# 128 bytes of padding ahead of the weights' pool in a two-layer decoder trunk

## The chip, the cores and the metric

The kernel runs on one core of one Trainium2 chip. The metric is the device time of one execution in microseconds. Three runs of the kernel before took 1982.12 to 1982.59 us, the median is 1982.57 us.

## What is computed

Two layers over x of 512 tokens by 1024 features, in float32. Each layer adds half a SwiGLU, then a mixer, then half a SwiGLU; each works on the RMS-normed x.

```python
for l in range(DEPTH):
    h = _rmsnorm(x, ffn_pre_norm[l])
    x = x + 0.5 * _swiglu(h, ffn_pre_w_gate[l], ffn_pre_w_up[l], ffn_pre_w_down[l])
    h = _rmsnorm(x, mix_norm[l])
    if l % 2 == 0:
        x = x + _retention_dilated_mixer(h, ab_w_in[l // 2], ab_w_out[l // 2])
    else:
        x = x + _gla_mixer(h, gla_w_in[l // 2], gla_w_a2[l // 2], gla_b_a[l // 2], gla_w_out[l // 2])
    h = _rmsnorm(x, ffn_post_norm[l])
    x = x + 0.5 * _swiglu(h, ffn_post_w_gate[l], ffn_post_w_up[l], ffn_post_w_down[l])
return _rmsnorm(x, final_norm)
```

`_swiglu(h, wg, wu, wd)` is `(silu(h @ wg) * (h @ wu)) @ wd` with 2816 hidden features. The even mixer is retention and dilated attention, the odd one is gated linear attention; both begin with a projection of h and end with one of their concatenated heads.

## The kernel before

The 512 tokens lie along the free dimension, 128 features at a time along the partitions. x is 8 tiles of 128 x 512 (`keep`). Before each block `scaled` makes gain times x as a pair of fp32r tiles, `xgh` and `xgl`, whose sum is the float32 value; the row scale of the norm comes after the projection. Weights are loaded by SyncE's queue into `wraw` (128 x 1024, two buffers, 512 KB each) and split by `load_w` into `whi` (ScalarE, L89) and `wlo` (VectorE, L90), four buffers each; `weights` keeps up to three sets ahead of their use.

Every large product goes through `mm3`: for one 128-deep slice, three matmuls into one PSUM bank, high by high (L124), high by low (L125), low by high (L126). The first operand of a matmul (`lhsT`, 128 x 128) is stationary and is loaded into the array ahead of it; the second (`rhs`, 128 x 512) moves through it. In the profile's rows a matmul is written as output, moving tile, stationary tile: `pj<-xgh,whi` has `xgh` moving.

- `proj_steps` (SwiGLU's gate and up, most of the mixers' input): one weight tile of 128 x 1024 gives 128 outputs in 8 x 3 matmuls; its stationary slices lie 512 bytes apart; `xg` moves.
- `proj_n_steps` (the mixers' values): `xg` is stationary in slices of 128 tokens, halves of a weight tile move.
- `down` (the SwiGLU's second product): 22 x 3 matmuls for each of 8 output tiles; `acth` and `actl`, the split activations, move. The last output tile of the kernel is made in two halves of 256 tokens (`last_half`).
- `out_steps` (the mixers' output): `cath` and `catl` move.

The stages run in this order: SwiGLU, even mixer, SwiGLU, SwiGLU, odd mixer, SwiGLU. In each SwiGLU 44 output tiles of projections (gate and up, 22 each) come ahead of the 8 of `down`. In the mixers the projections of later heads are woven into the attention work by hand (`weave`, `fill`), and the norm's statistics are put off and issued between products (`hook`; `rows` makes the row scale with `diag` moving and `ones_r` stationary). The even mixer projects 8 + 8 + 4 tiles with `proj_steps`, the odd one 1 + 8 + 8.

The pools are laid out one after the other in each partition of SBUF, in the order in which `__init__` (L47) opens them: `const`, `keep`, `xg`, `wpool`, `misc`, and after those the pool of the stage that runs. In the program as built the tiles start at these bytes of a partition (several buffers of a tile follow each other at 2048 or 4096 bytes):

| tiles | first byte | modulo 2048 |
|---|---|---|
| `ones_r` | 17024 | 640 |
| x | 18304 | 1920 |
| `xgh`, `xgl` | 34688, 51072 | 1920 |
| `wraw`, `whi`, `wlo` | 67456, 75648, 92032 | 1920 |
| `diag`, `rrow`, `sq` | 108640, 112736, 118880 | 96 |
| `acth`, `actl` (each SwiGLU) | 135488, 180544 | 320 |
| `cath`, `catl` (even mixer) | 185664, 202048 | 1344 |
| `cath`, `catl` (odd mixer) | 191488, 207872 | 1024 |

The even mixer's pool is the largest and ends at byte 228672.

Of the kernel before, what the change touches and what calls it, by code (L numbers as in the profile page):

```python
# [45 lines left out]
class Trunk:  # L46
    def __init__(self, ctx, tc, a):  # L47
        self.tc, self.nc, self.a = tc, tc.nc, a
        pool = lambda name, **kw: ctx.enter_context(tc.tile_pool(name=name, **kw))
        self.const = pool("const", bufs=1)  # L50
        self.keep = pool("keep", bufs=1)
        self.xg = pool("xg", bufs=KD)
        self.wpool = pool("wpool", bufs=4)
        self.misc = pool("misc", bufs=1)
        self.n = 0
        self.plan, self.ready, self.pending = [], [], []
# [5 lines left out]
    @contextmanager  # L62
    def banks(self, **tags):
        """The PSUM banks of a phase, by purpose."""
        with self.tc.tile_pool(name=self.uid("ps"), bufs=1, space=PSUM, reuse_waits="tile") as self.ps:
            self.tags = tags
            yield
# [7 lines left out]

# [1 line left out]
    def weights(self):  # L77
        """The next weights of the plan, in halves."""
        while self.plan and len(self.ready) <= LOOK:
            self.ready.append(self.load_w(*self.plan.pop(0)))  # L80
        return self.ready.pop(0)
# [11 lines left out]
    def hook(self):  # L93
        """One of the steps put off, if any."""
        if self.pending:
            with self.tc.issue_after(self.last):
                self.pending.pop(0)()

    def fill(self, filler, us):
        """Of the filler, about this much work for the tensor engine."""  # L100
        while us > 0:
            t = next(filler, None)
            if t is None:
                return
            us -= t
# [4 lines left out]

# [1 line left out]
    def halves(self, pool, tag, src, bufs):  # L112
        """src (an SBUF or PSUM tile) as two parts of 12 significant bits each."""
        nc = self.nc
        hi = self.t2k(pool, tag + "h", F32R, bufs)
        lo = self.t2k(pool, tag + "l", F32R, bufs)
        nc.scalar.copy(out=hi, in_=src)  # L117
        nc.vector.tensor_tensor(out=lo, in0=src, in1=hi.bitcast(F32), op=ALU.subtract)  # L118
        return hi, lo

    def mm3(self, out, w, x, first, last):
        """out += w.T @ x with (hi, lo) pairs."""
        mm = self.nc.tensor.matmul
        mm(out, lhsT=w[0], rhs=x[0], start=first, stop=False)  # L124
        mm(out, lhsT=w[0], rhs=x[1], start=False, stop=False)  # L125
        self.last = mm(out, lhsT=w[1], rhs=x[0], start=False, stop=last).ins  # L126

# [1 line left out]
    def setup(self):  # L129
# [33 lines left out]

# [1 line left out]
    def scaled(self, k, idx):  # L165
        """gain * x[k] in halves."""
        nc = self.nc
        g = self.gain[:, idx * KD + k: idx * KD + k + 1]
        hi = self.t2k(self.xg, "xgh", F32R)
        lo = self.t2k(self.xg, "xgl", F32R)  # L170
        nc.scalar.activation(out=hi, in_=self.x[k], func=AF.Copy, scale=g)
        nc.vector.scalar_tensor_tensor(out=lo, in0=self.x[k], scalar=g, in1=hi.bitcast(F32), op0=ALU.mult, op1=ALU.subtract)
        if k == 0:
            self.h = []
        self.h.append((hi, lo))

    def prep(self, k, idx):
        """From x[k]: gain * x in halves, and the squares into their sum."""
        self.scaled(k, idx)
        self.squares(k)  # L180
# [13 lines left out]
    def rstd_cols(self, cols, parts, n, out, nt=NT):  # L194
        """cols: PSUM [P, nt]; sums over the partitions of parts, by token; out = (mean + eps)^-0.5."""
        nc = self.nc
        for t in range(nt):
            for i, p in enumerate(parts):
                nc.tensor.matmul(cols[:, t:t + 1], lhsT=p[:, t * P:(t + 1) * P], rhs=self.ones[:, 0:1],  # L199
                                 start=i == 0, stop=i == len(parts) - 1)  # L200
        v = self.t2k(self.misc, "var", bufs=2, shape=[P, NT])
        nc.vector.tensor_scalar(out=v[:, :nt], in0=cols[:, 0:nt], scalar1=1.0 / n, scalar2=EPS, op0=ALU.mult, op1=ALU.add)
        nc.gpsimd.tensor_tensor(out=out[:, :nt], in0=v[:, :nt], in1=self.mhalf[:, 0:nt], op=ALU.pow)

    def rows(self, cols, tag, nt=NT):
        """[P, nt] values by token -> PSUM [P, nt * P], the same row in every partition, by exact halves."""
        nc = self.nc
        ps = self.psum(tag)
        half = self.t2k(self.misc, "colh", F32R, bufs=2, shape=[P, 2, NT])
        ident = self.ident.unsqueeze(1).broadcast_to([P, nt, P])  # L210
        nc.vector.tensor_copy(out=half[:, 0, :nt], in_=cols[:, :nt])
        nc.vector.tensor_tensor(out=half[:, 1, :nt], in0=cols[:, :nt], in1=half[:, 0, :nt].bitcast(F32), op=ALU.subtract)
        for i in range(2):
            diag = self.t2k(self.misc, "diag", F32R, bufs=2)
            nc.vector.tensor_tensor(out=split2(diag[:, :nt * P]), in0=ident, in1=half[:, i, :nt].bitcast(F32).unsqueeze(2).broadcast_to([P, nt, P]),
                                    op=ALU.mult)
            nc.tensor.matmul(ps[:, :nt * P], lhsT=self.ones_r, rhs=diag[:, :nt * P], start=i == 0, stop=i == 1)  # L217
        return ps
# [9 lines left out]

# [1 line left out]
    def proj_steps(self, done):  # L230
        """One 128-wide tile of outputs, transposed: PSUM [outputs, tokens], before the row scale."""
        w = self.weights()
# [16 lines left out]
    def proj_n_steps(self, tags, done):  # L249
        """512 outputs, tokens on partitions: 4 PSUM tiles, before the row scale."""  # L250
        ps = [self.psum(t) for t in tags]
# [14 lines left out]
    def out_steps(self, order, early, tags, idx):  # L266
        """The mixer's output projection; the first tiles wait with the last of cat."""
        nc = self.nc
# [21 lines left out]

# [1 line left out]
    def ffn(self, nxt):  # L292
# [45 lines left out]
    def last_half(self, d, ws, act, ts):  # L338
        """The end of the trunk for half of the tokens: the last tile of x, the final norm, the output."""
        nc = self.nc  # L340
# [25 lines left out]

# [1 line left out]
    def rotate(self, pool, ps, cos, sin, out, shift):  # L368
        """out = ps * cos + (ps with its rotary halves exchanged) * sin."""
        nc = self.nc  # L370
# [19 lines left out]
    def centered(self, pool, ps, t, width):  # L390
        """v * rstd less its mean over each head's width, from one PSUM tile of proj_n."""
        nc = self.nc
# [10 lines left out]
    def norm_steps(self, pool, outs, gates, cat, sq_tag, sq_bufs):  # L403
        """outs: PSUM tiles [e, tokens] of one head, with zero mean over e; cat: their index in cat."""
        nc = self.nc
# [174 lines left out]
    def retention(self, pool, qk, v, gates, need, more):  # L580
        """Emits all but the end of the last head's norm, which it returns."""
        nc = self.nc
# [37 lines left out]

# [1 line left out]
    def mixer_odd(self, nxt):  # L622
# [3 lines left out]
        with tc.tile_pool(name="odd", bufs=1, reuse_waits="tile") as pool, self.banks(pj=3, sc=3, o=2):  # L626
# [26 lines left out]
            def cums(h):  # L653
# [6 lines left out]
                nc.scalar.activation(out=e2, in_=b, func=AF.Exp, scale=-1.0)  # L660
                # In the place of the column that is exp(0), the first half's decay came.
                mid, end = slice(P // 2 - 1, T, P), slice(P - 1, T, P)
# [45 lines left out]
    def gla(self, pool, h, q, k, v, ex, tri, gates):  # L708
# [8 lines left out]
        for c in range(NT):  # L717
            nc.tensor.matmul(sc[:, sl[c]], lhsT=k[:, sl[c]], rhs=q[:, sl[c]], start=True, stop=True)
        # Of the upper right quarter of each block nothing is read: its exponents may be out of range.
        st = self.t2k(pool, "st", bufs=2)  # L720
# [72 lines left out]
def constants():  # L793
    """Tables that follow from the shapes alone."""
    f32 = np.float32
# [33 lines left out]
def layout(x, ffn_pre_norm, ffn_pre_w_gate, ffn_pre_w_up, ffn_pre_w_down, mix_norm, ab_w_in, ab_w_out, gla_w_in, gla_w_a2,  # L829
           gla_b_a, gla_w_out, ffn_post_norm, ffn_post_w_gate, ffn_post_w_up, ffn_post_w_down, final_norm):  # L830
    def tiles(w):
        """[K, N] -> [N/128, 128 (K within), K/128 * 128 (N within)]"""
        k, n = w.shape
        return w.reshape(k // P, P, n // P, P).transpose(2, 1, 0, 3).reshape(n // P, P, k)

    def wide(w):
        """[1024, 512] -> [4, 128 (K within), 2 * 512]"""
        return w.reshape(KD // 2, 2, P, T).transpose(0, 2, 1, 3).reshape(KD // 2, P, 2 * T)
# [39 lines left out]
```

## Time and profile before

| | |
|---|---|
| median of three runs | 1982.57 us |
| span of the profiled execution, first to last instruction | 1979.8 us |
| median less span | 2.8 us |
| TensorE matmuls busy | 1962.6 us, 99% |
| VectorE, ScalarE busy | 45%, 31% |
| mean HBM rate | 92 GB/s |

The page states no time for the profiled execution other than its span. To read it: matmuls overlap in the records (each one's modelled end lies behind the next one's start), so TensorE is shown busy almost without a gap, and the mean of one says less than the distance between two starts in the timeline. The span is 40 slices of 49.5 us; the granted clock is 9 tenths or more in all of them.

### The profile page before, as it was taken

How to read it: one execution, taken by the hardware profiler on the slowest of the kernel's cores; microseconds unless marked ns; L12 is line 12 of the kernel's file. 1: busy time of each engine (PE TensorE's matmuls, PEld its weight loads, DVE VectorE, ACT ScalarE, POOL GpSimd, SP SyncE). 2: the span in 40 equal slices, each digit the busy share in tenths (PEclk: the TensorE clock that was granted, in tenths of full speed). 3: DMA queues.
4: the chain of work that ended last, by engine and by line, in shares of the span. 5: the costliest groups of instructions: out<-in, count | busy, mean ns of one | idle time of the engine just before them, and what ended most of it. 6: DMA issues, size and time to landing. Idle time of an engine off the chain costs nothing.

```text
span 1979.8 us, 21475 instructions
## 1 busy us (share of the span) xinstructions
PE 1962.6 (99%) x8822; PEld 1593.8 (81%) x8822; DVE 900.2 (45%) x1238; ACT 611.9 (31%) x813; POOL 96.7 (5%) x69
## 2 busy tenths in 40 slices
PE   8999999999999999999999999999999999999998
PEld 7888888877777888888888888888788888888887
DVE  6444433444565544443334444333456564444323
ACT  5332222233332332222223323222424243323221
POOL 1000001100001200000110000011000020000010
PEclk9999999999999999999999999999999999999999
DMA  5333222421121322333332323323222133322222
GB/s 172 96 96 96 94 97 89 139 77 63 54 70 49 117 96 96 96 95 97 95 98 96 96 96 96 92 95 101 92 78 72 54 117 96 96 96 95 97 88 72
DMA packets 54548, 183.38 MB, mean 93 GB/s; under 512 B 6177, under 2 KB 8481, under 8 KB 54450
## 3 DMA queue, kind: packets, MB, share of 16 engines
q1 hardware_dynamic: 51408, 177.76, 28.0%
q10 hardware_dynamic: 3042, 4.26, 0.7%
q8 instruction: 69, 1.13, 0.2%
q14 instruction: 29, 0.24, 0.0%
HBM read 179.89 MB, written 2.10 MB: 92 GB/s over the span
## 4 chain that ended last, share of the span: by engine, by line
PE 98%; issue 0%; DVE 0%; DMA 0%; POOL 0%; ACT 0%; POOLq 0%; DVEq 0%; SPq 0%
PE pj L124 31%; PE pj L126 30%; PE pj L125 30%; PE sc L519 1%; PE o L547 1%; PE sc L199 1%; PE sc L594 0%; PE tp L535 0%; PE sc L217 0%; PE o L751 0%; PE o L744 0%; PE sc L733 0%; DMA wraw<-in_w_gu 0%; PE tp L603 0%; PE o L124 0%
## 5 line engine op out<-in xcount | busy, mean ns | idle before, releaser
L89 ACT CAST whi<-wraw 128x1024 fp32r<-128x1024 f32 (+1 forms) x341 | 352.0, 1033 | 1125.8 <-PE pj L125 669.0
L124 PE MATMUL pj<-xgh,whi 128*128 128x512 f32 x1704 | 677.6, 398 | 6.9 <-ACT whi L89 6.9
L126 PE MATMUL pj<-xgh,wlo 128*128 128x512 f32 x1704 | 664.9, 390 | 0.0
L125 PE MATMUL pj<-xgl,whi 128*128 128x512 f32 x1704 | 664.7, 390 | 0.0
L90 DVE TENSOR_TENSOR wlo<-wraw,whi 128x1024 fp32r<-128x1024 f32 (+1 forms) x341 | 413.1, 1212 | 306.1 <-ACT whi L89 305.0
L124 PEld LDWEIGHTS pj<-xgh,whi 128*128 128x128 f32 x1704 | 320.6, 188 | 83.5 <-issue 12.1
L126 PEld LDWEIGHTS pj<-xgh,wlo 128*128 128x128 f32 x1704 | 320.4, 188 | 67.9 <-DVE wlo L90 0.8
L125 PEld LDWEIGHTS pj<-xgl,whi 128*128 128x128 f32 x1704 | 320.9, 188 | 63.9 <-issue 1.0
L124 PE MATMUL pj<-acth,whi 128*128 128x512 f32 (+1 forms) x726 | 281.0, 387 | 0.0
L126 PE MATMUL pj<-acth,wlo 128*128 128x512 f32 (+1 forms) x726 | 280.9, 387 | 0.0
L125 PE MATMUL pj<-actl,whi 128*128 128x512 f32 (+1 forms) x726 | 280.9, 387 | 0.0
L302 DVE TENSOR_TENSOR us<-pj,rrow 128x512 f32<-128x512 f32 x88 | 60.8, 691 | 272.3 <-PE pj L126 272.3
L126 PEld LDWEIGHTS pj<-acth,wlo 128*128 128x128 f32 x726 | 135.8, 187 | 31.8
L125 PEld LDWEIGHTS pj<-actl,whi 128*128 128x128 f32 x726 | 135.8, 187 | 31.6
L124 PEld LDWEIGHTS pj<-acth,whi 128*128 128x128 f32 x726 | 135.8, 187 | 31.5
L189 POOL TENSOR_TENSOR sqa<-sqa,sq 128x512 f32<-128x512 f32 x41 | 70.6, 1722 | 1426.7 <-issue 798.1
L300 DVE TENSOR_TENSOR gs<-pj,rrow 128x512 f32<-128x512 f32 x88 | 60.8, 691 | 173.7 <-PE pj L126 173.7
L117 ACT CAST acth<-us 128x512 fp32r<-128x512 f32 x88 | 55.0, 625 | 61.1 <-DVE us L303 61.1
L303 DVE TENSOR_TENSOR us<-us,gs 128x512 f32<-128x512 f32 x88 | 60.9, 693 | 9.4 <-ACT gs L301 0.8
L325 DVE SCALAR_TENSOR_TENSOR x<-pj,x 128x512 f32<-128x512 f32 x31 | 21.5, 693 | 93.0 <-PE pj L126 93.0
L118 DVE TENSOR_TENSOR actl<-us,acth 128x512 fp32r<-128x512 f32 x88 | 60.4, 686 | 4.9 <-ACT acth L117 4.8
L301 ACT ACTIVATE gs<-gs 128x512 f32<-128x512 f32 x88 | 55.3, 630 | 4.2 <-DVE gs L300 4.2
(164 smaller groups left out, 1172.2 us busy)
## 6 DMA issues: line engine op xcount, KB each, us to landing
wraw<-in_w_gu SPq DMA_DIRECT2D x176, 512.0 KB, 3.4
wraw<-in_w_down SPq DMA_DIRECT2D x64, 448.0 KB, 3.2
wraw<-in_w_down SPq DMA_DIRECT2D x32, 512.0 KB, 3.4
wraw<-in_w_dqk SPq DMA_DIRECT2D x8, 512.0 KB, 3.4
wraw<-in_w_rqk SPq DMA_DIRECT2D x8, 512.0 KB, 3.4
wraw<-in_w_eo SPq DMA_DIRECT2D x8, 512.0 KB, 3.6
wraw<-in_w_gr SPq DMA_DIRECT2D x8, 512.0 KB, 3.4
wraw<-in_w_gv SPq DMA_DIRECT2D x8, 512.0 KB, 3.4
```

The source lines that it names most:

```text
L89: self.halved = nc.scalar.copy(out=hi[:, :cols], in_=raw[:, :cols]).ins
L90: nc.vector.tensor_tensor(out=lo[:, :cols], in0=raw[:, :cols], in1=hi[:, :cols].bitcast(F32), op=ALU.subtract)
L117: nc.scalar.copy(out=hi, in_=src)
L118: nc.vector.tensor_tensor(out=lo, in0=src, in1=hi.bitcast(F32), op=ALU.subtract)
L124: mm(out, lhsT=w[0], rhs=x[0], start=first, stop=False)
L125: mm(out, lhsT=w[0], rhs=x[1], start=False, stop=False)
L126: self.last = mm(out, lhsT=w[1], rhs=x[0], start=False, stop=last).ins
L189: nc.gpsimd.tensor_tensor(out=self.sqacc, in0=self.sqacc, in1=sq, op=ALU.add)
L300: nc.vector.tensor_tensor(out=gs, in0=g, in1=self.rrow, op=ALU.mult)
L301: nc.scalar.activation(out=gs, in_=gs, func=AF.Silu)
L302: nc.vector.tensor_tensor(out=us, in0=u, in1=self.rrow, op=ALU.mult)
L303: nc.vector.tensor_tensor(out=us, in0=us, in1=gs, op=ALU.mult)
```

## The change

A pool `gap` with one tile of 128 x 32 float32 values, 128 bytes of each partition, is opened between `xg` and `wpool`. Nothing writes or reads it. `const`, `keep` (x) and `xg` stay where they are, everything behind moves by 128 bytes: modulo 2048 the weights go from 1920 to 0, `diag`, `rrow` and `sq` from 96 to 224, `act` from 320 to 448, `cat` from 1344 to 1472 in the even mixer and from 1024 to 1152 in the odd one. The diff also takes out docstrings and comments, which is left out here.

```diff
@@ -50,6 +50,8 @@
         self.const = pool("const", bufs=1)
         self.keep = pool("keep", bufs=1)
         self.xg = pool("xg", bufs=KD)
+        self.gap = pool("gap", bufs=1)
+        self.gap.tile([P, 32], F32, name="gap", tag="gap")
         self.wpool = pool("wpool", bufs=4)
         self.misc = pool("misc", bufs=1)
         self.n = 0
```

## Rows read from the trace of the kernel before

**Rows 1.** the page, section 1: span, busy us (share) and instructions of each engine

```profile
span 1979.8 us, 21475 instructions
...
PE 1962.6 (99%) x8822; PEld 1593.8 (81%) x8822; DVE 900.2 (45%) x1238; ACT 611.9 (31%) x813; POOL 96.7 (5%) x69
```

**Rows 2.** the page, section 4: the chain that ended last, by engine and by line

```profile
PE 98%; issue 0%; DVE 0%; DMA 0%; POOL 0%; ACT 0%; POOLq 0%; DVEq 0%; SPq 0%
PE pj L124 31%; PE pj L126 30%; PE pj L125 30%; PE sc L519 1%; PE o L547 1%; PE sc L199 1%; PE sc L594 0%; PE tp L535 0%; PE sc L217 0%; PE o L751 0%; PE o L744 0%; PE sc L733 0%; DMA wraw<-in_w_gu 0%; PE tp L603 0%; PE o L124 0%
```

**Rows 3.** TensorE's two longest waits: who waited for whom, us in total, times, longest us

```profile
PE pj L124 <- ACT whi L89: 6.9, 1, 6.9
PE sc L217 <- DVE diag L215: 2.7, 3, 1.8
```

**Rows 4.** stretches: us; busy (instructions) of PE, PEld, DVE, ACT, POOL; clock, DMA share, GB/s

```profile
100.00:200.00 100.00, 100.00 (x443) 82.84 (x442) 46.81 (x56) 29.79 (x37) 0.00 (x0) 1.00 0.31 96
410.00:610.00 200.00, 199.75 (x933) 145.29 (x931) 101.53 (x206) 72.57 (x143) 3.23 (x3) 1.00 0.20 64
```

**Rows 5.** TensorE's groups by line and shape, count | busy us, mean ns | idle before

```profile
L124 PE MATMUL pj<-xgh,whi 128*128 128x512 f32 x1704 | 677.6, 398 | 6.9 <-ACT whi L89 6.9
...
L124 PE MATMUL pj<-acth,whi 128*128 128x512 f32 x682 | 268.7, 394 | 0.0
...
L124 PE MATMUL pj<-whi,xgh 128*128 128x512 f32 x112 | 45.3, 404 | 0.0
...
L124 PE MATMUL o<-whi,xgh 128*128 128x512 f32 x16 | 6.3, 395 | 0.0
```

**Rows 6.** timeline, `xg` moving: start us, us, instruction; 36 steps, and one weight load

```profile
99.63 0.39 PE L125 MATMUL pj<-xgl,whi 128*128 128x512 f32 x1
...
100.08 0.39 PE L124 MATMUL pj<-xgh,whi 128*128 128x512 f32 x1
100.08 0.19 PEld L125 LDWEIGHTS pj<-xgl,whi 128*128 128x128 f32 x1
...
107.79 0.39 PE L125 MATMUL pj<-xgl,whi 128*128 128x512 f32 x1
```

**Rows 7.** timeline of TensorE, `act` moving: first and last of 52 steps

```profile
299.83 0.39 PE L126 MATMUL pj<-acth,wlo 128*128 128x512 f32 x1
...
311.96 0.39 PE L124 MATMUL pj<-acth,whi 128*128 128x512 f32 x1
```

**Rows 8.** timeline of TensorE, even `cat` moving: first and last of 30 steps

```profile
644.83 0.39 PE L125 MATMUL pj<-catl,whi 128*128 128x512 f32 x1
...
651.83 0.39 PE L125 MATMUL pj<-catl,whi 128*128 128x512 f32 x1
```

**Rows 9.** timeline of TensorE, odd `cat` moving: first and last of 41 steps

```profile
1593.81 0.40 PE L124 MATMUL pj<-cath,whi 128*128 128x512 f32 x1
...
1603.34 0.40 PE L126 MATMUL sc<-cath,wlo 128*128 128x512 f32 x1
```

**Rows 10.** timeline of TensorE, weights moving (`proj_n_steps`): first and last of 47 steps

```profile
1413.18 0.39 PE L125 MATMUL pj<-wlo,xgh 128*128 128x512 f32 x1
...
1423.84 0.39 PE L124 MATMUL pj<-whi,xgh 128*128 128x512 f32 x1
```

**Rows 11.** timeline of TensorE, `xg` after an interruption: steps 0, 10 and 22

```profile
380.15 0.39 PE L125 MATMUL pj<-xgl,whi 128*128 128x512 f32 x1
...
382.46 0.39 PE L126 MATMUL pj<-xgh,wlo 128*128 128x512 f32 x1
...
385.18 0.39 PE L126 MATMUL pj<-xgh,wlo 128*128 128x512 f32 x1
```

**Rows 12.** timeline of TensorE: the two `diag` matmuls and the next start

```profile
385.41 0.63 PE L217 MATMUL sc<-diag,ones_r 128*128 128x512 f32 x2
385.88 0.39 PE L124 MATMUL pj<-xgh,whi 128*128 128x512 f32 x1
```

## The prediction

> **What bounds the kernel now.** I read the page's busy times first: TensorE (PE) is busy for 1962.6 of 1979.8 us, VectorE for 45% and ScalarE for 31% [rows 1]. The chain that ended last is TensorE for 98%, and three lines carry 91% of the span, L124, L125 and L126, the three matmuls of `mm3` [rows 2]. TensorE's longest waits are one of 6.9 us for the first weights and 2.7 us in three for `diag` [rows 3]. In a steady stretch of the SwiGLU's projections VectorE is busy for 47 us of 100 and ScalarE for 30, with the clock granted in full [rows 4]. So nothing that feeds TensorE is late, and the time of the kernel is a count of matmuls times the pace from one start to the next.
>
> The mean durations do not give that pace: 390 ns stand for a matmul whose successor starts after some 227 [rows 5, 6]. The reader has to take the starts from the timeline, a first and a last matmul with the number of steps between.
> - `xg` moving, weights stationary: 36 steps from 99.63 to 107.79, 8.16 us, 226.7 ns [rows 6].
> - `act` moving, weights stationary: 52 steps from 299.83 to 311.96, 12.13 us, 233.3 ns [rows 7].
> - `cat` of the even mixer moving: 30 steps, 7.00 us, 233.3 ns [rows 8].
> - `cat` of the odd mixer moving: 41 steps, 9.53 us, 232.4 ns [rows 9].
> - weights moving, `xg` stationary (`proj_n_steps`): 47 steps, 10.66 us, 226.8 ns [rows 10].
>
> All are the same instruction, 128x512 in fp32r at a granted clock of 1.00, the level of 2.4 GHz, at which 512 columns take 213.3 ns. Each pays 13 to 20 ns more, and how much goes with the tile that is read. The load of the next stationary tile starts with the running matmul (100.08 and 100.08) [rows 6], so two reads of SBUF lie beside each other. After an interruption the `xg` stream needs some ten matmuls to find its pace: 10 steps from 380.15 to 382.46 at 231, then 12 steps to 385.18 at 226.7 [rows 11]. It falls into a rhythm, and the rhythm differs by tile. This is what a change of offsets can touch.
>
> **The change part by part.** *The tile itself.* `gap` is written and read by nothing: no instruction, no transfer, no wait is added or moved, and no queue is passed. Cost 0. The docstrings and comments that go cost 0 too. The largest pool ends at byte 228672, so 128 more bytes need no other allocation; the pools keep their order.
>
> *Other engines' accesses.* ScalarE and VectorE read and write `wraw`, `whi`, `wlo`, `act` at other offsets. Even 10% on their 47 and 30 us of 100 [rows 4] would stay under TensorE's time; I price it at 0, and the cover is that slack. Were it gone, one wait as long as the 6.9 us of the first weights [rows 3] would show at L124. The transfers of weights land behind the same slack: 0.
>
> *TensorE's pace.* This is the whole question, and the trace shows none of the new pairs of offsets for the large stage. I write the offsets modulo 512 where they concern weights, since the stationary slices of one weight tile lie 512 bytes apart and the `xg` stream keeps one pace over all of them. The distance from the stationary slice to the moving tile is 0 for `xg` (1920 and 1920), 448 for `act` (320 and 1920), 448 for the even `cat` (1344 and 1920), 128 for the odd `cat` (1024 and 1920), and 0 for the moving weights. Sorted by it the paces are 226.7 and 226.8 at distance 0, 233.3 twice at 448, 232.4 at 128. After the change weights go to 0, `act` to 448, `cat` to 1472 and 1152, `xg` stays at 1920: the distances of `act` and of both `cat` stay as they are, that of `xg` becomes 384, that of the moving weights 128.
>
> So if the pair of reads sets the pace, the only streams that change are those that are now at the one fast pace. For `xg` at 384 no row exists. It is bounded below by the present 226.7 (no loss; a gain is the third rival), above by the slowest back-to-back pair of that size, the two `diag` matmuls, 385.41 to 385.88, 235 ns each [rows 12]. The nearest row is distance 448, 233.3 ns [rows 7]; I take that, 6.6 ns more. For the moving weights at 128 the row is the odd `cat`, 232.4 ns, 5.6 more [rows 9].
>
> The counts: 1704 x 3 = 5112 matmuls with `xg` moving [rows 5]. The mixers' part of them is 20 + 17 output tiles of 8 x 3, 888; the four SwiGLU stages have 4 x 44 x 8 x 3 = 4224. With the weights moving there are (112 + 16) x 3 = 384 [rows 5]. The SwiGLU stages run almost wholly at the settled pace: 4224 x 6.67 = 28.2 us. In the mixers the matmuls are woven three or six at a time among others (933 matmuls of all kinds in 200 us [rows 4]) and a stream that restarts is at 231 anyway [rows 11], so I count half: 444 x 6.67 = 3.0 and 192 x 5.6 = 1.1; between none and all of it lie 0 and 8 us. Sum 32.3 us. The 2046 matmuls of `act` (682 x 3 [rows 5]) cost the same as now, and so do the `cat` ones.
>
> The profiled span of 1979.8 becomes 2012.1. The page gives no other time of that execution; its span is 2.8 us under the median of 1982.57, and I keep those 2.8 outside: 2014.9, say 2015. With 231 for `xg`, the pace of a stream that never settles, it would be 4224 x 4.3 = 18.2 and 2.8 from the mixers, 2003.6; with 235, 4224 x 8.3 = 35.1 and some 5.3, 2023. What is late next is still TensorE; nothing else comes near.
>
> **The rivals.** *First: the start of the moving tile alone sets the pace* (faster). The rows allow it as well: 1920 goes with 226.7, 320 and 1344 with 233.3, 1024 with 232.4, and the stationary offset was never varied against a fixed moving one. Then `xg` stays, and `act` at 448 and the even `cat` at 1472, 64 bytes from where the fast tiles start modulo 512, could fall to 226.7: 2046 x 6.67 = 13.6 and 192 x 6.67 = 1.3 saved. Moving weights, now at 0, would run like a tile at 1024, 232.4: half of 384 x 5.6, 1.1 to 2.2 lost. That is 12.7 saved, 1970; with the odd `cat` falling too (192 x 5.7 = 1.1) and the moving weights unhurt 1966.6. It decides from a pace of `act` under 231.4: 2 ns off 2046 matmuls are the 0.2% (4 us) that a measurement of this kernel can tell from no change. Against it: a pace that takes ten matmuls to settle [rows 11] looks like two streams that fall into step, more than like a toll on one.
>
> *Second: nothing happens.* The difference of paces could belong to something that goes with the tiles but not with their last bits, such as their place: `act` and `cat` all lie above byte 131072, `xg` and the weights below. Against it: the two `cat` tiles lie in one region and differ by 0.9 ns [rows 8, 9]. That `gap`, which nobody touches, gets no room is part of this case. 1982.6, within 1 us.
> The Trainium skill, "TensorE: Matmul & The Clock Gate", section "Step-by-step: what each phase is for", gives TensorE two independent SBUF read ports and says that loading the next tile's weights takes no bandwidth from the running matmul; by that rule the distance of the two tiles costs nothing and the time stays at 1982.6. The trace doesn't bear it out in full: the same page's warm gap is about 216 ns for 512 columns, and no steady stream here is under 226.7.
>
> *Third: the new distance is better than 0* and `xg` settles one step of 6.67 ns lower, at 220: 28.2 and 4.1 us saved, 1950. For it, that 213.3 leaves room; against it, that none of five streams is there.
> *Fourth: it settles a step above all that the trace shows*, at 240, 13.3 over: 56.3 and 8.2, 2047. Against it likewise that no stream is there.
>
> **How the numbers follow.** The pair of reads decides and `xg` loses its pace: 0.42, 2015, with a range of its own of 2003 to 2023. The moving start alone: 0.20, 1970. Nothing: 0.24, 1982.6. The better step: 0.08, 1950. The worse: 0.06, 2047. Losing outweighs gaining because `xg` now has the best pace of all and the other known distances are all worse. From 1966 to 2023 the first three lie, 0.86; their edges take that to about 8 in 10. Faster by over 0.2% are the first and the third rival, 0.28; within 0.2% the second, 0.24; slower the forecast and the fourth, 0.48.
>
> **What the profile of the changed kernel would show.** By my forecast the starts of `xg` matmuls in the first SwiGLU stage lie 231 to 235 ns apart, those of `act` still 233.3, even `cat` 233.3, odd `cat` 232.4; the settled stretch of the moving weights is near 232; the matmul counts, the waits and the busy times of the other engines stay, and the added time lies evenly over the four SwiGLU stages' projections, about 7 us in each. By the first rival `xg` stays at 226.7 and `act` moves. I am wrong if the distance matters only in a coarser or finer way than I read (then `xg` at 384 is as good as at 0), or if the new offset of the weights itself, 0 modulo 2048, changes the paces of `act` and `cat` as well, which the sum holds fixed.

## The result and the profile after

The changed kernel takes 2011.2 us (median of four runs, 2008.88 to 2013.59) against 1982.43 us: the ratio is 1.0146, 95% interval 1.0132 to 1.0161. The change makes the kernel slower by 28.8 us. The profiled execution took 2013.59 us with a span of 2011.6, so 2.0 us lie outside the span.

The page of the changed kernel: span, busy times, and the chain's share by line (L126 to L128 are the three matmuls of `mm3`, L124 to L126 before).

```profile
span 2011.6 us, 21475 instructions
...
PE 1994.6 (99%) x8822; PEld 1602.0 (80%) x8822; DVE 898.7 (45%) x1238; ACT 610.9 (30%) x813; POOL 97.3 (5%) x69
...
PE pj L126 31%; PE pj L128 30%; PE pj L127 30%; PE sc L521 1%; PE o L549 1%; PE sc L201 1%; PE sc L596 0%; PE tp L537 0%; PE sc L219 0%; PE o L753 0%; PE o L746 0%; PE sc L735 0%; DMA wraw<-in_w_gu 0%; PE tp L605 0%; PE o L126 0%
```

As in [rows 1, 2], TensorE is busy for 99%, with the same 8822 matmuls, and the chain is TensorE's. It is busy for 32.0 us more, the span is 31.8 longer. The paces come from the timeline again, a first and a last matmul and the steps between. `xg` moving, 33 steps, answering to [rows 6]:

```profile
100.11 0.39 PE L127 MATMUL pj<-xgl,whi 128*128 128x512 f32 x1
...
107.78 0.39 PE L127 MATMUL pj<-xgl,whi 128*128 128x512 f32 x1
```

7.67 us for 33 steps, 232.4 ns against 226.7. `act` moving, 55 steps, answering to [rows 7]:

```profile
299.42 0.39 PE L126 MATMUL pj<-acth,whi 128*128 128x512 f32 x1
...
312.25 0.40 PE L127 MATMUL pj<-actl,whi 128*128 128x512 f32 x1
```

12.83 us, 233.3 ns, as before. The even `cat`, 32 steps, and the odd `cat`, 43 steps, answering to [rows 8, 9]:

```profile
652.32 0.39 PE L126 MATMUL pj<-cath,whi 128*128 128x512 f32 x1
...
659.79 0.39 PE L128 MATMUL pj<-cath,wlo 128*128 128x512 f32 x1
```

```profile
1619.25 0.40 PE L126 MATMUL pj<-cath,whi 128*128 128x512 f32 x1
...
1629.25 0.40 PE L127 MATMUL sc<-catl,whi 128*128 128x512 f32 x1
```

7.47 us and 10.00 us, 233.4 and 232.6 ns, as before within the resolution of a start. The weights moving, 46 steps, answering to [rows 10]:

```profile
1433.11 0.40 PE L128 MATMUL pj<-whi,xgl 128*128 128x512 f32 x1
...
1443.84 0.40 PE L126 MATMUL pj<-whi,xgh 128*128 128x512 f32 x1
```

10.73 us, 233.3 ns against 226.8. So the two streams whose distance changed lost the fast pace, and the three whose distance stayed kept theirs, although `act` and `cat` moved by 128 bytes as well. (Distance here is the start of the moving tile less the start of the stationary slice, in bytes.)

The steps themselves, in ns from one start to the next, say more than their mean. The first line is the odd `cat` of the kernel before, from 1581.73 us on, the second `xg` of the changed kernel, from 100.11 us on:

```
before, odd cat:  228 230 233 240 233 231 231 229 230 232 241 233
after, xg:        228 230 233 240 233 231 231 229 230 232 241 233
```

It is the same rhythm; it is seven steps long (1626.7 ns, 232.4 in the mean), and the lines show it once and the most of a second time, with the rounding of a start. `xg` now lies 128 bytes below the weights, the odd `cat` lay 128 bytes above, modulo 512.

Summed over all starts in the trace, `xg` moving costs 1206.6 us against 1179.9, 26.7 more: 24.5 in the 4224 matmuls of the SwiGLU stages (6.6 in the first, 6.0 in each of the others) and 2.2 in the 888 of the mixers. The moving weights cost 94.4 against 89.7, 4.7 more, and `act` 477.4 both times.

Not all of the 4.7 is pace. In the odd mixer the clock falls in this execution, which it does not in the profile of the kernel before. First the stretch of the kernel before, then three of the changed one: length, busy us and instructions of PE, PEld, DVE, ACT and POOL, granted clock, DMA share, GB/s:

```profile
1406.00:1413.00 7.00, 7.00 (x30) 5.22 (x29) 0.00 (x0) 6.68 (x6) 0.00 (x0) 1.00 0.26 75
```

```profile
1410.00:1426.00 16.00, 16.00 (x68) 11.85 (x67) 7.16 (x11) 5.97 (x9) 1.02 (x1) 1.00 0.20 73
1426.00:1433.00 7.00, 7.00 (x16) 4.75 (x15) 0.00 (x0) 6.34 (x6) 0.00 (x0) 0.52 0.24 75
1433.00:1440.00 7.00, 7.00 (x31) 5.60 (x31) 3.71 (x5) 2.19 (x2) 0.00 (x0) 0.99 0.11 28
```

The timeline at that place: the eight matmuls of the low rank on 17 rows (L646), then the first with the weights moving.

```profile
1423.02 2.84 PE L646 MATMUL sc<-wa,low 17*128 17x512 f32 x6
1425.70 1.36 PE L646 MATMUL o<-wa,low 17*128 17x512 f32 x2
1426.99 0.79 PE L126 MATMUL pj<-whi,xgh 128*128 128x512 f32 x1
1427.58 0.63 PE L127 MATMUL pj<-wlo,xgh 128*128 128x512 f32 x1
1428.01 0.63 PE L128 MATMUL pj<-whi,xgl 128*128 128x512 f32 x1
```

The records give the clock at 0.5, 1.2 GHz, from 1426.25 for 6.83 us. A matmul of 512 columns takes 427 ns there (1427.58 to 1428.01 is 0.43) in place of 233, so of the 6.83 us some 3.1 are lost. Two of the four runs came to 2013.3 and 2013.6, the other two to 2008.9 and 2009.1; these 4.5 us are more than the 3.1, and what the rest is was not looked at.

### The profile page after: what moved, and what is told of

Read it like the earlier page. It is cut to its first block, busy times and chain, and to the rows that moved or that the text cites. A ratio compares the mean times of both kernels' runs of the same rounds, so it can differ in the third digit from the quotient of the medians.

```text
span 2011.6 us, 21475 instructions
## 1 busy us (share of the span) xinstructions
PE 1994.6 (99%) x8822; PEld 1602.0 (80%) x8822; DVE 898.7 (45%) x1238; ACT 610.9 (30%) x813; POOL 97.3 (5%) x69
## 4 chain that ended last, share of the span: by engine, by line
PE 98%; issue 0%; DVE 0%; DMA 0%; POOL 0%; ACT 0%; POOLq 0%; DVEq 0%; SPq 0%
PE pj L126 31%; PE pj L128 30%; PE pj L127 30%; PE sc L521 1%; PE o L549 1%; PE sc L201 1%; PE sc L596 0%; PE tp L537 0%; PE sc L219 0%; PE o L753 0%; PE o L746 0%; PE sc L735 0%; DMA wraw<-in_w_gu 0%; PE tp L605 0%; PE o L126 0%
## 5 line engine op out<-in xcount | busy, mean ns | idle before, releaser
L126 PE MATMUL pj<-xgh,whi 128*128 128x512 f32 x1704 | 686.2, 403 | 6.7 <-ACT whi L91 6.7
L127 PE MATMUL pj<-xgl,whi 128*128 128x512 f32 x1704 | 673.5, 395 | 0.0
L128 PE MATMUL pj<-xgh,wlo 128*128 128x512 f32 x1704 | 673.4, 395 | 0.0
L126 PEld LDWEIGHTS pj<-xgh,whi 128*128 128x128 f32 x1704 | 321.8, 189 | 90.6 <-issue 12.1
L128 PEld LDWEIGHTS pj<-xgh,wlo 128*128 128x128 f32 x1704 | 321.6, 189 | 75.5 <-DVE wlo L92 0.8
L126 PE MATMUL pj<-acth,whi 128*128 128x512 f32 (+1 forms) x726 | 282.1, 389 | 0.0
L128 PE MATMUL pj<-acth,wlo 128*128 128x512 f32 (+1 forms) x726 | 282.1, 389 | 0.0
L128 PEld LDWEIGHTS pj<-acth,wlo 128*128 128x128 f32 x726 | 136.5, 188 | 31.0
L126 PEld LDWEIGHTS pj<-acth,whi 128*128 128x128 f32 x726 | 136.5, 188 | 30.9
```

## The experiments

Theory 1: in a stream of `mm3` the distance between moving tile and stationary slice, modulo some power of two, sets the pace. The rivals are the moving start alone, the stationary start alone, and the place in SBUF.

**A grid of distances, with nothing else running.** The trunk is replaced by 30 streams of 96 matmuls, each on its own line, 26 of 512 columns and 4 of 256. In a stream the moving tile starts at byte m and the stationary slice at byte w.

```diff
+def s_m64_w128(nc, ps, mv, wt):
+    for g in range(GROUPS):
+        out = ps.tile([P, T], F32, tag="ps", name="s_m64_w128_%d" % g, bufs=4)
+        for i in range(3 * KD):
+            k = i // 3
+            nc.tensor.matmul(out[:, :512], lhsT=wt[:, 32 + k * P:32 + (k + 1) * P],
+                             rhs=mv[:, 16 + k * T:16 + k * T + 512], start=i == 0, stop=i == 3 * KD - 1)
```

> This kernel leaves the trunk out: it only runs streams of matmuls and stores x. Each of 30 streams is 96 matmuls of 128x512 in fp32r, moving tiles at byte m modulo 2048, stationary slices at byte w modulo 512; every stream has its own line, its pace is read from the starts in the timeline. Theory 1, the distance m - w modulo 256 sets the pace: every pair with m = w runs at 226.7 ns wherever it lies, every pair at distance 128 at 232.4, every pair at distance 192 (64 below) at 233.3, and m of 256, 512 or 1024 over w = 0 like 0; distance 64 is in no trace yet, 227 to 235. Rival, the start of the stationary slice sets the pace: all streams with w = 128 run at 226.7 and all with w = 0 near 232.4, whatever m is. Rival, the start of the moving tile: all with m = 128 at 226.7, all with m = 64 at 233.3, whatever w is. If a distance of 16 or 32 bytes shows a pace below 226.7, there is something to be had beyond the kernel before.

TensorE's groups by line: one line is one stream; busy us runs from its first start to its last end, so the pace is busy less the mean of one, by 95.

```profile
L166 PE MATMUL s_m_w<-mv,wt 128*128 128x512 f32 x96 | 22.6, 396 | 0.0
...
L118 PE MATMUL s_m_w<-mv,wt 128*128 128x512 f32 x96 | 22.6, 394 | 0.0
...
L206 PE MATMUL s_m_w<-mv,wt 128*128 128x512 f32 x96 | 22.5, 395 | 0.0
...
L126 PE MATMUL s_m_w<-mv,wt 128*128 128x512 f32 x96 | 22.5, 395 | 0.0
L182 PE MATMUL s_m_w<-mv,wt 128*128 128x512 f32 x96 | 22.4, 394 | 0.0
...
L54 PE MATMUL s_m_w<-mv,wt 128*128 128x512 f32 x96 | 22.1, 391 | 0.0
...
L134 PE MATMUL s_m_w<-mv,wt 128*128 128x512 f32 x96 | 22.1, 391 | 0.0
...
L190 PE MATMUL s_m_w<-mv,wt 128*128 128x512 f32 x96 | 21.9, 389 | 0.0
...
L102 PE MATMUL s_m_w<-mv,wt 128*128 128x512 f32 x96 | 21.9, 389 | 0.0
L142 PE MATMUL s_m_w<-mv,wt 128*128 128x512 f32 x96 | 21.9, 389 | 0.0
...
L230 PE MATMUL s_m_w_n<-mv,wt 128*128 128x256 f32 x96 | 11.7, 283 | 0.0
...
L254 PE MATMUL s_m_w_n<-mv,wt 128*128 128x256 f32 x96 | 11.1, 276 | 0.0
```

For instance L118 (m 192, w 0): (22.6 - 0.394) / 95 = 233.7 ns, and L102 (m 128, w 128): (21.9 - 0.389) / 95 = 226.4, each to 1 ns. The starts of the last 65 steps of each stream give it finer:

| distance m - w modulo 256 | pairs (m, w) | ns, 512 columns |
|---|---|---|
| 0 | (0, 0), (64, 64), (128, 128), (192, 192), (256, 0), (512, 0), (1024, 0) | 226.7 each |
| 16 | (16, 0) | 231.7 |
| 32 | (32, 0) | 233.4 |
| 64 | (64, 0), (128, 64), (192, 128), (0, 192), (320, 0) | 228.8 to 228.9 |
| 96 | (96, 0) | 233.4 |
| 128 | (128, 0), (192, 64), (0, 128), (64, 192), (384, 0) | 232.4 to 232.5 |
| 160 | (160, 0) | 234.2 |
| 192 | (192, 0), (0, 64), (64, 128), (128, 192) | 233.3 to 233.4 |
| 224 | (224, 0) | 233.3 |

The sixteen pairs of the 64-byte grid fall into four classes by their distance alone; rows and columns of the grid (moving start, stationary start) hold every pace each. Both rivals on one start alone fall. The period is 256 bytes: 256 and 512 are as good as 0, and 320 and 384 are as 64 and 128. None of the nine distances beats 0. With 256 columns the order is another: 120.0 ns at distance 0, 117.8 at 64, 118.7 at 128, 113.3 at 192 (L230 and L254 are the first and the last of these).

**The padding ahead of everything.** `xg` and the weights move together.

```diff
+        self.gap = pool("gap", bufs=1)
+        self.gap.tile([P, 32], F32, name="gap", tag="gap")
         self.const = pool("const", bufs=1)
```

> The padding of 128 bytes lies ahead of the first pool instead: the weights stand at 0 modulo 2048 and act and cat where the change put them, but xg moves along to 0. Theory 1 (distance): xg is at distance 0 again, 226.7 ns, and the kernel takes 1982.4 us, within 2. Rival (the weights' own start, 0 modulo 2048, is the slow one): xg stays at 232.4 and the kernel takes some 2009 us. Rival (moving start alone): xg at 0 like the odd cat at 1024, 232.4, 2009 us.

1982.46 us, ratio to the kernel before 1.0002 (0.9992 to 1.0011). `xg` in the timeline, 37 steps:

```profile
99.73 0.39 PE L127 MATMUL pj<-xgl,whi 128*128 128x512 f32 x1
...
108.12 0.39 PE L128 MATMUL pj<-xgh,wlo 128*128 128x512 f32 x1
```

8.39 us, 226.8 ns: the weights stand where the change put them, and the pace is the old one. The loss of the changed kernel is not in the weights' new offset.

**256 bytes in place of 128.**

```diff
+        self.gap = pool("gap", bufs=1)
+        self.gap.tile([P, 64], F32, name="gap", tag="gap")
         self.wpool = pool("wpool", bufs=4)
```

> The padding of the change is 256 bytes in place of 128: xg at 1920, weights at 128, act at 576, cat at 1600 and 1280 modulo 2048. Theory 1 with a period of 256: xg at 226.7 ns, 1982.4 us, within 2. With a period of 512 or more the distance of 256 is a new one: 227 to 235 ns, up to 2020 us. Rival (the weights' own start modulo 256, 128 as before): 1982.4 as well; e2 tells these two apart.

1982.34 us, ratio 1.0001 (0.9991 to 1.0011). `xg`, 37 steps:

```profile
99.74 0.39 PE L127 MATMUL pj<-xgl,whi 128*128 128x512 f32 x1
...
108.13 0.39 PE L128 MATMUL pj<-xgh,wlo 128*128 128x512 f32 x1
```

226.8 ns again. The same padding, twice as long, costs nothing: the period of 256 bytes holds in the kernel.

**Only what lies behind the weights.** The other part of the change alone: `act` and `cat` move by 128 bytes, the weights stay.

```diff
         self.wpool = pool("wpool", bufs=4)
+        self.gap = pool("gap", bufs=1)
+        self.gap.tile([P, 32], F32, name="gap", tag="gap")
         self.misc = pool("misc", bufs=1)
```

> The padding of 128 bytes lies behind the pool of weights: weights and xg stay at 1920, act goes to 448, cat to 1472 and 1152 modulo 2048 as in the changed kernel. By the grid of distances modulo 256 (0: 226.7, 64: 228.9, 128: 232.4, 192: 233.4 ns; at 256 columns 64: 117.8, 192: 113.3): xg stays at 226.7, act at distance 64 goes from 233.3 to 228.9, 2046 x 4.45 = 9.1 us saved, the even cat 192 x 4.5 = 0.9, the odd cat at distance 0 192 x 5.7 = 1.1, the last output tile loses 132 x 4.4 = 0.6: 10.5 us saved, 1971.8, within 2. Rival, the moving start alone sets the pace of act (448 as in the changed kernel, where it ran at 233.3): act stays at 233.3 and the time at 1982, within 2.

1971.62 us, ratio 0.9957 (0.9943 to 0.9971); 1971.8 was worked out from the grid. `act`, 58 steps:

```profile
298.82 0.39 PE L128 MATMUL pj<-acth,wlo 128*128 128x512 f32 x1
...
312.10 0.39 PE L126 MATMUL pj<-acth,whi 128*128 128x512 f32 x1
```

13.28 us, 229.0 ns. `act` stands at the same 448 as in the changed kernel, where it runs at 233.3: its own start does not set its pace. Of the change, the moved activations alone would have gained; together with the moved weights their distance is as before and they gain nothing.

**Everything at distance 0.** The version that the theory asks for.

```diff
         self.wpool = pool("wpool", bufs=4)
+        self.gap = pool("gap", bufs=1)
+        self.gap.tile([P, 16], F32, name="gap", tag="gap")
         self.misc = pool("misc", bufs=1)
...
+            pool.tile([P, 16], F32, name="gap2", tag="gap2")
             cum = pool.tile([P, P], F32, name="cum", tag="cum")
```

> The kernel before, with 64 bytes of padding behind misc and 64 more ahead of the odd mixer's pool: xg and weights stay at 1920, act goes from 320 to 384, cat from 1344 to 1408 and from 1024 to 1152 modulo 2048, all at distance 0 modulo 256 from the weights. Theory 1 with a period of 256: act and cat run at 226.7 ns like xg; 2046 x 6.67 = 13.6, 192 x 6.67 = 1.3 and 192 x 5.7 = 1.1 us are saved, 1966.4 us, faster than both kernels. With a period of 512 the odd cat stays near 232, 1967.5. Rival (the place above byte 131072 makes act slow, not its offset): 1982.4, and act stays at 233.3.

1969.32 us (1966.13 to 1970.15), ratio 0.9931 (0.9916 to 0.9946), faster than both kernels. `act`, 59 steps:

```profile
298.83 0.39 PE L128 MATMUL pj<-acth,wlo 128*128 128x512 f32 x1
...
312.20 0.39 PE L127 MATMUL pj<-actl,whi 128*128 128x512 f32 x1
```

13.37 us, 226.6 ns, so a tile above byte 131072 runs as fast as one below: the rival of the place falls. Over the trace `act` costs 463.8 us, 13.6 less, as worked out. Against that the last output tile, 256 columns at distance 0, costs 15.9 against 15.1 us. The median lies 2.9 us above the 1966.4 that was worked out, the lowest run meets it; the profiled one, 1968.8, has 3.4 us at half the clock in the odd mixer, of which some 1.6 are lost.

**The clock.** In the odd mixer `wa` and `low` get 128 rows, with zeros in `wa` below row 17; once in the kernel with everything at distance 0, once in the changed kernel.

```diff
-            wa = pool.tile([GLA_LOW + 1, T], F32, name="wa", tag="wa")
-            nc.scalar.dma_start(out=wa, in_=a["w_a2"])
-            low = pool.tile([GLA_LOW + 1, T], F32, name="low", tag="low")
+            wa = pool.tile([P, T], F32, name="wa", tag="wa")
+            nc.gpsimd.memset(wa, 0.0)
+            nc.scalar.dma_start(out=wa[:GLA_LOW + 1], in_=a["w_a2"])
+            low = pool.tile([P, T], F32, name="low", tag="low")
```

> The kernel of e4, and in the odd mixer wa and low have 128 rows, zeros below row 17 of wa, so that the eight matmuls between 17 and 128 rows of the gate's low rank use all rows. In the profiles of the changed kernel and of e4 the granted clock falls to 0.5 behind these matmuls (for 6.8 and 3.4 us), in that of the kernel before it does not. If the small matmuls bring the fall on, it is gone: all runs near the lowest of e4, 1966.1, and less spread, no row at 0.5 between start and end. If the fall has another cause, runs stay between 1966 and 1970 and the profile may show it.

> The changed kernel with wa and low on 128 rows likewise. Its four runs came to 2008.9, 2009.1, 2013.3 and 2013.6 us, and the profile of a slow one has 6.8 us at half the clock behind those matmuls. If they bring the fall on, all runs are near 2009; the pace of xg stays at 232.4. If not, runs at 2013 stay.

With everything at distance 0: 1966.54 us (1965.67 to 1966.67), ratio 0.9919 (0.9905 to 0.9934), the lowest median here. The changed kernel: 2009.41 us (2008.89 to 2009.49), ratio 1.0136 (1.0121 to 1.0151). The same stretch of the changed kernel with wide `wa` that fell to 0.52 above, and its eight matmuls on 128 rows:

```profile
1426.00:1433.00 7.00, 7.00 (x31) 5.61 (x30) 0.00 (x0) 6.68 (x6) 0.00 (x0) 1.00 0.24 75
```

```profile
1422.68 2.74 PE L647 MATMUL sc<-wa,low 128*128 128x512 f32 x6
1425.26 1.02 PE L647 MATMUL o<-wa,low 128*128 128x512 f32 x2
```

The clock stays at 1.00. The matmuls follow each other by 429 ns as on 17 rows, but two short delays around them are gone: from the first of the eight to the second matmul behind them it takes 3.67 us, in the kernel before, on 17 rows at the full clock, 3.96. None of these eight runs lies apart from the others of its kernel, while 7 of the 13 runs of the changed kernel, of the one with distance 0 and of the one with `act` moved lie 2 to 6 us above the lowest of theirs.

The slower pace is not what brings the fall on. The profile of the kernel with the padding ahead of everything, at the old pace, has it too, 3.41 us long:

```profile
1407.00:1411.00 4.00, 4.00 (x12) 3.10 (x11) 0.00 (x0) 3.97 (x3) 0.00 (x0) 0.57 0.14 55
```

And of 39 runs taken together, 19 of the kernel before and 10 each of the two paddings that kept its pace, 5 lie some 3 us above the median of theirs. That the 17-row matmuls bring the fall on fits all of this, but is not shown: it comes in three of six profiles with them and in none of two without, and the edit also takes away the two delays.

**One distance, two rhythms.** The profile of the changed kernel with wide `wa` shows something else. Its weights, moving in the odd mixer over the same `xg` slices as above and at the same offsets, 42 steps:

```profile
1433.09 0.39 PE L126 MATMUL pj<-whi,xgh 128*128 128x512 f32 x1
...
1442.85 0.39 PE L126 MATMUL pj<-whi,xgh 128*128 128x512 f32 x1
```

9.76 us, 232.4 ns in the rhythm of seven steps; in the changed kernel the same matmuls run in turns of 229 and 238 ns, 233.3 in the mean, and so does the first such stretch of both kernels (403 us). The odd `cat` is at distance 128 in the kernel before, in the changed one and in the two whose padding kept the old time (e2, e3): it has 232.4 in the first two and 233.3 in the last two, although e2 has `cat` and weights at the very bytes of the changed kernel. `xg` of the changed kernel has 233.3 in 5 of 287 settled stretches of 14 steps and 232.4 in the others. So at distance 128 a stream can settle in either of two rhythms. What picks one was not tried; between 226.7 at distance 0 and either of them the gap is much larger than between the two.

**Is it the read of the next slice?** Streams alone again: stationary slices of 128, 64 and 32 columns, and offsets that alternate so that a matmul's own pair and the pair of its moving tile with the next slice differ.

```diff
+            nc.tensor.matmul(out[:64, :], lhsT=wt[:, k * P:k * P + 64], rhs=mv[:, 16 + k * T:16 + k * T + T], ...)
...
+            k, m, w = i // 3, (0, 32)[i % 2], (32, 0)[i % 2]
```

> Leaves the trunk out again: 16 streams of 96 matmuls of 512 columns. The first 12 have stationary slices of 128, 64 and 32 columns at distances 0, 64, 128 and 192. If the read of the next stationary slice is what holds the running matmul up, the time over 213.3 ns shrinks with the slice: from 13.3 to 20 at 128 columns to about half at 64 and a quarter at 32, and the spread between distances shrinks with it. If the extra time is a toll on the moving read or a fixed cost of a change of weights, the paces stay at 226.7 to 233.4 whatever the slice. The last four streams alternate offsets so that a matmul's own pair and the pair of its moving tile with the next slice differ: own 0 next 128, own 128 next 0, own 0 next 64, own 64 next 0. If the load beside the running matmul decides, own 128 next 0 and own 64 next 0 run at 226.7 and own 0 next 128 near 232.4, own 0 next 64 near 228.9; if the pair of one matmul decides, the other way round.

TensorE's groups by line, as in the grid. L38 and L46 are 128 columns at distances 128 and 192, L54 and L78 64 columns at 0 and 192, L86 and L110 32 columns at 0 and 192, L118 own 0 next 128, L126 own 128 next 0.

```profile
L46 PE MATMUL s_c_m<-mv,wt 128*128 128x512 f32 x96 | 22.6, 394 | 0.0
L78 PE MATMUL s_c_m<-mv,wt 128*64 128x512 f32 x96 | 22.5, 395 | 0.0
L38 PE MATMUL s_c_m<-mv,wt 128*128 128x512 f32 x96 | 22.5, 395 | 0.0
...
L110 PE MATMUL s_c_m<-mv,wt 128*32 128x512 f32 x96 | 22.4, 394 | 0.0
...
L86 PE MATMUL s_c_m<-mv,wt 128*32 128x512 f32 x96 | 22.4, 394 | 0.0
...
L54 PE MATMUL s_c_m<-mv,wt 128*64 128x512 f32 x96 | 22.2, 392 | 0.0
L126 PE MATMUL s_own_next<-mv,wt 128*128 128x512 f32 x96 | 22.2, 392 | 0.0
...
L118 PE MATMUL s_own_next<-mv,wt 128*128 128x512 f32 x96 | 22.1, 390 | 0.0
```

| columns of the slice | distance 0 | 64 | 128 | 192 |
|---|---|---|---|---|
| 128 | 226.7 | 228.9 | 232.4 | 233.3 |
| 64 | 230.0 | 228.3 | 229.3 | 232.7 |
| 32 | 231.7 | 231.7 | 230.8 | 231.7 |

This went as none of the theories said. A shorter slice narrows the spread between distances, from 6.6 ns to 4.4 and to 0.9, so the stationary read has a part in it; but the time over 213.3 ns does not shrink with the slice, it stays at 17 to 18 ns in the mean. And own 0 next 128 runs at 228.3, own 128 next 0 at 230.0, own 0 next 64 and own 64 next 0 at 231.7: neither pair decides by itself.

**Other offsets for the low tiles.** `mm3`'s order, the low moving tile at byte a, the low weights at byte b, the high ones at 0; then one operand alone alternating.

```diff
+            k, m, w = i // 3, (0, 16, 0)[i % 3], (0, 0, 32)[i % 3]
+            nc.tensor.matmul(out, lhsT=wt[:, w + k * P:w + (k + 1) * P], rhs=mv[:, m + k * T:m + (k + 1) * T], ...)
```

> Leaves the trunk out: 22 streams of 96 matmuls of 128x512. The first 16 have mm3's order (high moving with high weights, low moving with high weights, high moving with low weights), the low moving tile at byte a and the low weights at byte b modulo 256, the high ones at 0. The last six alternate one operand alone between two offsets. If a matmul's own pair, or the pair of the moving tile with the next slice, set each step by itself, a stream's pace is the mean of the grid's paces over its three pairs: 226.7 only at a = b = 0, and 227.4 to 231 elsewhere. If the streams settle as a whole, as the alternating ones of e6 suggest (own 0 next 128 at 228.3, own 128 next 0 at 230.0), paces are no such means, and one below 226.7 may be among them; that would give a version with other offsets for the low tiles. I expect none under 226.7.

The slowest, the fastest other than a = b = 0 among the sixteen, and the fastest of the six (a 128 with b 0, a 192 with b 0, moving 0 and 192 in turn):

```profile
L86 PE MATMUL s_xl_wl<-mv,wt 128*128 128x512 f32 x96 | 22.6, 395 | 0.0
...
L118 PE MATMUL s_xl_wl<-mv,wt 128*128 128x512 f32 x96 | 22.1, 390 | 0.0
L166 PE MATMUL s_m_w<-mv,wt 128*128 128x512 f32 x96 | 21.9, 388 | 0.0
```

Their paces are 233.4, 228.9 and 226.7; the means of the grid's paces over the three pairs would be 228.6 for the first and 228.9 for the second, and over the two pairs 230.0 for the third. One agrees, two don't, so a stream settles as a whole: a stream whose pairs have several distances has a pace that the grid doesn't give. None of the 22 is under 226.7.

## Why the prediction was right

*The bound.* TensorE's pace times its count is the time: the same counts, 32.0 us more of TensorE, 31.8 us more of span.

*The parts priced at nothing.* The tile, the transfers, ScalarE and VectorE: the waits of TensorE stay (6.7 us for the first weights, [rows 3] has 6.9), and `act`'s sum over the trace is the same to 0.1 us.

*The distance decides.* This was chosen over the moving start and over no effect with rows that could not part them. The grid parts them, the two kernels with the same weights' offset and other paces (e2) or the same `act` offset and another pace (e5) do so in the trunk. It does not fix the pace to the nanosecond: at 128 it leaves two rhythms 0.9 ns apart. The first rival's forecast that `act` would fall to 226.7 at 448 was wrong; its time, 1970, is near that of e5, for another reason. The Trainium skill, "TensorE: Matmul & The Clock Gate", section "Step-by-step: what each phase is for", says that loading the next weights takes no read bandwidth from the running matmul. The grid, where one stream runs at a time and nothing else, has 226.7 to 234.2 ns by the distance of the two tiles, so for fp32r at 512 columns the place of the stationary tile does touch the running stream; whether it does so through the read bandwidth no run shows.

*The terms.* Forecast and measured in the profiled execution:

| term | forecast, us | measured, us |
|---|---|---|
| `xg` in the SwiGLU stages | 28.2 | 24.5 |
| `xg` in the mixers | 3.0 | 2.2 |
| moving weights | 1.1 | 2.0, and 2.7 more at half the clock |
| `act`, `cat` | 0 | 0 to 0.1 |
| last output tile, 256 columns | not in the sum | 0.5 |
| outside the span | 2.8 | 2.0 |

The first term was mis-sized by the choice of a row. I took distances modulo 512, where 384 is nearest to 448, 233.3 ns [rows 7]; the period is 256, and 384 is then 128, the odd `cat`'s 232.4 [rows 9], which was the other row at hand: 4224 x 5.7 = 24.1. That the wrong row was off by 0.9 ns only is partly luck: the rows at hand couldn't tell the period, and with `xg` at distance 64 the loss would have been 2.2 ns a step, by the grid.

The mixers' two terms lie within the 0 to 8 us that I had allowed. The moving weights settle at 233.3 where I had 232.4, in the second of the two rhythms at distance 128, and for more than the half that I counted. The last output tile keeps its distance, 192, and still costs 0.5 us more: at 256 columns most of its steps take 117.8 ns, where the kernel before had 113.3, and some 20 of them still do here, so there too one distance has two rhythms.

That the clock could fall in the odd mixer was nowhere in the sum; it costs the profiled run some 3.1 us. The changed kernel with wide `wa`, whose profile has no such fall, lies 27.0 us above the kernel before (2009.41 less 1982.38); a part of the difference to 28.8 is the wide `wa`'s own, whose profile has 110.7 us in all matmuls outside the four kinds of stream, against 111.6 before. The forecast of 2015 was 3.8 us too high for the median, and 5.6 too high for the version without the fall. The whole range, 1966 to 2023, took in a gain and no change as well; it is the paces that bear the forecast out, more than the time's lying in it.

*What I had said would make it wrong* is half true: 0 and 384 are not alike, but the pattern repeats every 256 bytes where I had read it over 512. With 256 bytes in place of 128 nothing would have been lost.

## What to carry to other kernels

Where TensorE bounds a kernel, read its pace from start to start for each stream of matmuls: the same instruction ran at 226.7 or 233.3 ns here by where its tiles lie. For fp32r streams of 512 columns with a new slice of 128 columns for every matmul, put moving and stationary tiles at equal offsets modulo 256 bytes; 128 bytes of padding in one place cost 28.8 us, 64 bytes in each of two others saved 13.0. This holds as far as it was tried: distances in steps of 16 bytes, nine of them, one distance for all matmuls of a stream. For 256 columns measure again, the order of the distances is another.

## What the runs showed of the hardware that was not expected

The period is 256 bytes, and a distance of 16 bytes already costs 5 ns on top of 226.7. The settled rhythms are exact: 226.7 is 34 times 6.67 ns, a steady 233.3 is 35 times, and other distances run through two, three, four or seven unequal steps. One distance can have two rhythms: 232.4 and 233.3 at 128, and at 192 with 256 columns 113.3 and 117.8. Why this is so, and why a slice of 32 columns costs no less, stays open; that the two reads of SBUF meet is fitted by the narrowing spread but not shown.

With eight matmuls on 17 rows, 3.6 us from the first start to the next stream's, the clock fell to half in three of six profiles, for 3.4 us in two and for 6.8 in one, although TensorE had work all the time; on 128 rows, 3.0 us, it did so in neither of two. That the few rows are the reason is not shown.
